# A two-layer decoder trunk: pre-norm weights as one spread row, compressed values without a masked copy, and a merged transition between the layers

## The chip, the cores and the metric

The kernel runs on one core of one Trainium2 chip. The metric is the device time of one execution in microseconds (us). Several runs are taken, and their median is given. The engines are called TensorE (PE; its weight loads PEld), VectorE (DVE), ScalarE (ACT), GpSimd (POOL) and SyncE (SP, which here only issues transfers).

## The reference

Two layers over 512 tokens of width 1024, float32. Each adds a normed mixer to its input:

```python
def rmsnorm(x, g):
    return x * lax.rsqrt(jnp.mean(x * x, axis=-1, keepdims=True) + EPS) * g

for i in range(2):
    u = rmsnorm(x, norm_pre[i])
    y = nsa_mixer(u, ...) if i == 0 else diff_mixer(u, ...)
    x = x + rmsnorm(y, norm_post[i])
```

`nsa_mixer` projects `u @ w_in` (3632 columns) into queries of 16 heads in 4 groups, three pairs of keys and values, gates and a SiLU path `z`. It adds three softmax branches (over 31 compressed blocks, over selected blocks, over a window) and ends with `@ w_out`. The compressed branch is what the change touches:

```python
p_c = softmax(where(m_c, q @ k_cmp + bias_c, NEG)) * any(m_c)
o_c = einsum('bgjqc,bcgd->bqgjd', p_c, v_cmp)
```

`diff_mixer` projects `u @ w_in` (4096 columns) into `q, k, v, z`, takes the difference of two softmax maps per head, norms per head, and ends with `@ w_out`.

## The kernel before

Tokens lie in four blocks of 128 (`NT = 4`), the width in eight blocks of 128 (`KD = 8`). A float32 product is made of three fp32r products: each operand is split into a rounded high half (`hi`, L99, an ACT copy, or a POOL operation) and a low half (`lo`, L104, a subtraction), and PE adds high x high, low x high and high x low.

Weights come through a stream (`Stream`, L108): `load` fetches a block of at most 512 KB on SP's queue into one of two `wraw` buffers, and `split` makes its halves in pieces. `split` takes the engines from `by`, two letters per piece, the first for the high half and the second for the low half (A is ACT, P is POOL, D is DVE). A block in `extra` is fetched into two `P` tiles and split into `wx` tiles. `SPD` (L43) holds the letters for the first block of `dv1`.

Projections are jobs. `mjob` gives columns x tokens. `tjob` (L205) gives tokens x columns; with `by_token` it goes through all of its weights for one token block before the next, and `evac` copies each token block's accumulator out of PSUM. Its accumulators come from PSUM banks by name: two `mm`, two `S`, three `T`, one `av`. The framework orders a writer of a bank behind earlier readers of it, also where two accumulators share the bank.

The first stage loads token block 0, the two halves of the pre-norm weights (L298, 256 KB each, one row of memory read into 128 partitions) and the first two weight blocks on SP's queue, then token blocks 1 to 3 (L610). `WARM` matmuls on a zeroed tile run meanwhile (L305). `prenorm` (L355) makes, per token block, two squares with their sums on ACT (L361), the partial sum (`part_sum`, L331), the root and one step of refinement (`row_rstd`, L340), and the normed row (L373). Its `turn` transposes the row on PE and splits it. After each token block eight steps of the job queue follow: those of `vs`, and then of `vw`.

In the attention of layer 0, `Cmp` (L881) is the compressed branch of a head group. Its `t` makes the values masked per head: a DVE multiply (L918), an ACT copy and a DVE subtraction.

The transition lies in a region where PE's order is that of the program (L1081 to L1103). The job `o1` is the second half of layer 0's output projection. When a token block of it is done, `after0` (L1065) calls `prenorm` for layer 1 with `EARLY`: there the product with the weights is POOL's (L364) and the scaling DVE's (L369). Block 1's transposes come before the last step of `o1` (`PRE1`). Then `SEQ` (L44) interleaves `dv0` (a), `dv1` (b) and the transposes of blocks 2 and 3 (p2, p3). `dv0` goes by token with two S banks for four token blocks. `tc.issue_after(i)` queues what is traced within it behind instruction `i`, on the engine of `i` and only there.

All other engines' orders, and PE's outside this region, are made by the framework at build time, by priority and a model of the times.

Of the kernel before, what the change touches and what calls it, by code (L numbers as in the profile page):

```python
# [18 lines left out]
S = 512  # L19
WARM = 7  # L20
EARLY = True
PRE1 = 29
# [20 lines left out]
SPD = ('PD',)*4  # L43
SEQ = 'a0 a1 p2 b0 b1 a2 p3 b2 a3 b3'.split()  # L44
# [24 lines left out]
def trunk(ctx: ExitStack, tc: tile.TileContext, x, table, npre, npost, w_in, pe_k, w1_k, w2_k,  # L69
# [135 lines left out]
    def tjob(name, w, width, col, n, evac, banks, cuts=((0, 4), (4, 4)), by_token=False):  # L205
        def run(i):
            bs = [bank(b) for b in banks]
            per = 4 // len(bs)
            acc = [bs[t // per][:, (t % per) * n:(t % per) * n + n] for t in range(NT)]
# [14 lines left out]
            if by_token:  # L224
                for ci in range(len(cuts)):
                    cut[ci] = ws.cut.pop(i + ci)
                for t in range(NT):
                    for ci in range(len(cuts)):
                        yield from part(ci, t)
                    evac(t, acc[t])  # L230
# [64 lines left out]
    load_x(0)  # L295
    gpre = [ptile() for _ in range(2)]
    for i in range(2):
        nc.sync.dma_start(gpre[i], drows(npre, i * 512, [[0, 128], [1, 512]]))  # L298
# [6 lines left out]
    for _ in range(WARM):  # L305
        nc.tensor.matmul(bank("T")[:, :256], BT[0][:, :128], BT[0][:, :256], start=True, stop=True)

# [47 lines left out]
    def prenorm(t, src, xn, grow, uh, ul, early):  # L355

        halves = (slice(0, 512), slice(512, 1024))
        ss = [small(1, tag="ss") for _ in range(2)]
        with tc.issue_after(T0["a"]) if "a" in T0 else ExitStack():
            for c, s in zip(halves, ss):  # L360
                nc.scalar.activation(pttile(F32) if early else xn[:, c], src[:, c], AF.Square, accum_out=s)  # L361
        if early:
            for c, g in zip(halves, grow):
                nc.gpsimd.tensor_tensor(xn[:, c], src[:, c], g, op=OP.mult)  # L364
        m0 = part_sum(ss[0])
# [9 lines left out]
        def turn():  # L375
            for i in range(2):
# [6 lines left out]
                x = hi(uh[:, i * 4:i * 4 + 4, cs], pv).ins  # L383
                T0["h"] = x
                if t == 0:
                    T0["a"] = x
# [153 lines left out]
    tjob("vs", w_in, NSA_IN, 1792, 256, evac_v(0), ("S", "S", "mm", "mm"), by_token=True)  # L540
# [50 lines left out]
    for n in range(4):  # L591
        tjob(f"dv{n}", dw_in, DIFF_IN, 2048 + n * 256, 256, evac_dv(n), (("S", "S"), ("mm", "mm"))[n % 2],
             by_token=n == 0)
# [70 lines left out]
    xn = slot("D", [128, NT, D])  # L664
# [216 lines left out]
    class Cmp:  # L881
# [22 lines left out]
        def t(self, i):  # L904
            g = self.g
            if True:
                p = bank("T")
                for qb in range(NT):
# [7 lines left out]
                vb = ptile()  # L916
                v3 = vb[:, 0:256].rearrange("p (h d) -> p h d", h=4)
                nc.vector.tensor_tensor(v3, T["vc"][:, g:g + 1, :].to_broadcast([128, 4, 64]),  # L918
                                        bmask[:, :, None].to_broadcast([128, 4, 64]), op=OP.mult)
                vt = pttile()  # L920
                hi(vt[:, 0:256], vb[:, 0:256])
                lo(vt[:, 256:512], vb[:, 0:256], vt[:, 0:256])
# [356 lines left out]
```

## Time and profile before

| | us |
|---|---|
| median of 3 runs | 663.3 |
| lowest and highest | 663.24, 665.05 |
| the profiled execution | 661.7 |
| its span, first to last instruction | 659.8 |

| engine | busy us | share of the span |
|---|---|---|
| PE | 635.3 | 96% |
| DVE | 413.7 | 63% |
| POOL | 401.3 | 61% |
| ACT | 340.3 | 52% |

Times in rows are us from the span's start. A row of the timeline names its start, its length, the engine, the line, the operation, the output and inputs with their size, the count of merged instructions, and in brackets the idle time before it with what ended it. The length of a merged row goes from the first start to the last end. A matmul's own length overlaps with its neighbours'. A row by stage gives the stretch, its length, the busy time of each engine, TensorE's granted clock as a share of 2.4 GHz, the DMA engines' busy share and GB/s.

### The profile page before, as it was taken

What the parts mean: (1) busy time and instruction counts of PE and PEld (TensorE: products, weight loads), DVE (VectorE), ACT (ScalarE), POOL (GpSimd) and SP (SyncE); (2) the same over time, 40 slices, a digit from 0 to 9 for tenths busy, and PEclk for the clock granted to TensorE, in tenths of its full rate; (3) what the DMA queues carried; (4) which work ended last, traced back from release to release, by engine and by line L of the source; (5) the groups of instructions that cost most, each with busy time, mean ns of one, the idle gap of its engine ahead of it and who ended that gap; (6) DMA issues with size and microseconds to landing.
All of it is one profiled execution on the core that took longest, in us unless ns stands there. A gap on an engine that the chain in (4) does not pass through costs nothing.

```text
span 659.8 us, 11242 instructions
## 1 busy us (share of the span) xinstructions
PE 635.3 (96%) x3773; PEld 555.5 (84%) x3773; DVE 413.7 (63%) x1188; ACT 340.3 (52%) x904; POOL 401.3 (61%) x675
## 2 busy tenths in 40 slices
PE   6999999999999999999999899999999998989996
PEld 5888888888788788888887899898987987879885
DVE  5611235678778978969878900236558668797634
ACT  6311234675767567768564311235564574668431
POOL 4778558777777587768586457948674563522300
PEclk8999999999999999999999899999999998999998
DMA  8565423213022111201852212322333232225302
GB/s 254 145 166 132 124 76 92 60 34 71 27 65 66 33 47 41 58 17 36 298 187 96 96 54 75 117 74 89 88 81 79 68 80 62 65 64 191 129 25 103
DMA packets 68989, 60.52 MB, mean 92 GB/s; under 512 B 3628, under 2 KB 60868, under 8 KB 68932
## 3 DMA queue, kind: packets, MB, share of 16 engines
q1 hardware_dynamic: 68212, 57.45, 29.9%
q10 hardware_dynamic: 720, 2.36, 0.9%
q8 instruction: 30, 0.49, 0.3%
q14 instruction: 27, 0.22, 0.1%
HBM read 55.04 MB, written 4.76 MB: 91 GB/s over the span
## 4 chain that ended last, share of the span: by engine, by line
PE 81%; DVE 11%; ACT 3%; DMA 3%; issue 2%; POOL 0%; SPq 0%; DVEq 0%; ACTq 0%; POOLq 0%
PE mm L198 31%; PE mm L218 12%; PE mm L467 6%; PE T L856 5%; PE av L870 5%; PE S L218 5%; PE S L801 4%; PE S L800 4%; PE S L467 3%; PE av L1166 2%; PE T L721 1%; DMA wraw<-in_nsa_w_in_dram 1%; PE T L1156 1%; DMA P<-in_nsa_w_out_dram 1%; DVE P L792 1%
## 5 line engine op out<-in xcount | busy, mean ns | idle before, releaser
L167 POOL TENSOR_TENSOR wlo<-wraw,whi 128x256 fp32r<-128x256 f32 (+2 forms) x247 | 184.2, 774 | 23.8 <-ACT whi L163 12.4
L165 POOL TENSOR_SCALAR whi<-wraw 128x256 fp32r<-128x256 f32 (+1 forms) x240 | 95.5, 424 | 111.9 <-PE mm L198 65.9
L794 ACT ACTIVATE P<-P,st 128x512 f32<-128x512 f32 (+3 forms) x192 | 107.5, 560 | 87.6 <-DVE st L792 86.7
L850 POOL TENSOR_SCALAR P<-P,st,gate 128x512 f32<-128x512 f32 (+3 forms) x128 | 80.1, 637 | 27.0 <-DVE st L847 24.9
L792 DVE CUSTOM_DVE_ANT_0 P<-S,BT 128x128 f32<-128x128 f32 (+2 forms) x144 | 59.7, 418 | 28.6 <-PE S L801 26.1
L198 PE MATMUL mm<-bigA,whi 128*128 128x512 f32 x192 | 77.4, 403 | 0.1
L198 PE MATMUL mm<-bigA,wlo 128*128 128x512 f32 x192 | 75.3, 392 | 0.0
L198 PE MATMUL mm<-bigB,whi 128*128 128x512 f32 x192 | 75.3, 392 | 0.0
L105 DVE TENSOR_TENSOR PT<-T,PT 128x512 fp32r<-128x512 f32 x84 | 56.9, 685 | 8.2 <-ACT PT L100 6.4
L870 PE MATMUL av<-PT,bigE 128*128 128x512 f32 x160 | 56.4, 417 | 1.2 <-DVE bigF L878 0.9
L105 DVE TENSOR_TENSOR stk<-mm,stk 64x512 fp32r<-64x512 f32 x32 | 22.0, 688 | 52.5 <-ACT stk L100 52.1
L198 PE MATMUL mm<-bigF,whi 128*128 128x512 f32 x128 | 51.9, 405 | 0.0
L856 PE MATMUL T<-ident,P 128*128 128x128 f32 x320 | 51.8, 272 | 0.0
L100 ACT ACTIVATE PT<-T 128x512 fp32r<-128x512 f32 x84 | 48.6, 592 | 6.0 <-PE T L856 3.9
L856 PEld LDWEIGHTS T<-ident,P 128*128 128x128 f32 x320 | 41.0, 140 | 12.3 <-issue 0.4
L100 ACT ACTIVATE stk<-mm 64x512 fp32r<-64x512 f32 x64 | 37.8, 591 | 25.8 <-PE mm L198 14.9
L198 PE MATMUL mm<-bigE,whi 128*128 128x512 f32 x128 | 50.8, 397 | 0.0
L198 PE MATMUL mm<-bigF,wlo 128*128 128x512 f32 x128 | 50.7, 396 | 0.0
L218 PE MATMUL mm<-whi,bigF 128*128 128x256 f32 x176 | 50.3, 287 | 0.1
L218 PE MATMUL mm<-wlo,bigF 128*128 128x256 f32 x176 | 50.0, 285 | 0.0
L218 PE MATMUL mm<-whi,bigE 128*128 128x256 f32 x176 | 49.6, 283 | 0.0
L198 PEld LDWEIGHTS mm<-bigB,whi 128*128 128x128 f32 x192 | 36.1, 188 | 8.1
(288 smaller groups left out, 1650.8 us busy)
## 6 DMA issues: line engine op xcount, KB each, us to landing
wraw<-in_diff_w_in_dram SPq DMA_DIRECT2D x31, 512.0 KB, 3.9
wraw<-in_nsa_w_in_dram SPq DMA_DIRECT2D x26, 512.0 KB, 4.1
BT<-rd SPq DMA_DIRECT2D x32, 128.0 KB, 3.4
wraw<-in_diff_w_out_dram SPq DMA_DIRECT2D x5, 512.0 KB, 4.0
bigF<-in_x_dram SPq DMA_DIRECT2D x4, 512.0 KB, 9.5
wraw<-in_nsa_w_out_dram SPq DMA_DIRECT2D x4, 512.0 KB, 3.4
bigD<-in_x_dram SPq DMA_DIRECT2D x4, 512.0 KB, 3.7
x1d<-bigD ACTq DMA_DIRECT2D x4, 512.0 KB, 4.9
```

Source lines behind the costliest of these rows:

```text
L100: return nc.scalar.activation(dst, src, AF.Copy, scale=scale)
L105: nc.vector.tensor_tensor(dst, src, h.bitcast(F32), op=OP.subtract)
L165: nc.gpsimd.tensor_scalar(h[:, a:b], v, 1.0, 0.0, op0=OP.mult, op1=OP.add)
L167: e.tensor_tensor(l[:, a:b], v, h[:, a:b].bitcast(F32), op=OP.subtract)
L198: T["mm"] = nc.tensor.matmul(p[:, a:b], wt[:, k, :], u[:, k, a:b], start=(k == 0 and j == 0), stop=(k == KD - 1 and j == 2)).ins
L218: nc.tensor.matmul(acc[t], u[:, k0 + k, t * 128:(t + 1) * 128], wt[:, k, :], start=(ci == 0 and k == 0 and j == 0 and t % per == 0), stop= ...
L467: nc.tensor.matmul(p, U[u][:, k, t * 128:(t + 1) * 128], wt[wi], start=start and j == 0, stop=stop and j == 2, skip_group_check=True)
L792: nc.vector.tensor_tensor_reduce(out=o, in0=i0, in1=b, op0=OP.add, op1=OP.min, scale=-1.0, scalar=BIG, accum_out=nm)
L794: nc.scalar.activation(pt[:, :n], pt[:, :n], AF.Exp, bias=nm, scale=-1.0, accum_out=den)
L850: NORM(nc, i, br, qb).tensor_scalar(self.P[i][:, :n], self.P[i][:, :n], st[:, 8 + i:9 + i], gate[:, NT - 1 - qb, c:c + 1], op0=OP.mult, op ...
L856: T["tmark"] = nc.tensor.transpose(p[:, j * 128:(j + 1) * 128], self.P[j][:, kb * 128:(kb + 1) * 128], ident).ins
L870: nc.tensor.matmul(av, T["V"][:, br, kb, g, :], p, start=(br == 0 and kb == 0 and j == 0), stop=(br == 1 and kb == qb and j == 1))
```

## The change

First stage: the pre-norm weights come as one row of 4 KB into partition 0 of the tile `xn`, through ACT's queue. Two matmuls with a row of ones spread it into the two `mm` banks, from which the multiply (L373) reads it. Token block 0 comes in two transfers. Two warm-up matmuls are left of seven. From block 1 on, one square of 1024 columns replaces two, and its partial sum falls away. `vs` takes its accumulators one at a time, all from the S banks.

Compressed values: four ACT copies scaled by a column of the mask and four DVE operations, each of 64 columns, replace the masked copy and its split.

Transition: the high halves of `dv1`'s first block go from POOL to ACT, the low ones from DVE to POOL. Block 1's transposes move from within `o1` to the head of `SEQ`. `dv0` has a bank of its own for each token block (S, T, S, S). POOL's work traced in the region is queued behind the last multiply (L364). The rule that queues later squares on ACT behind the split of block 0 is dropped.

```diff
--- before.py
+++ after.py
@@ -17,9 +17,8 @@
 AX = mybir.AxisListType
 
 S = 512
-WARM = 7
+WARM = 2
 EARLY = True
-PRE1 = 29
 ZE = 'gpsimd', 'vector'
 OB = (2,2,2)
 LAG = 1
@@ -40,8 +39,8 @@
 OPRE = 0
 ODELAY = 0
 QN = 1
-SPD = ('PD',)*4
-SEQ = 'a0 a1 p2 b0 b1 a2 p3 b2 a3 b3'.split()
+SPD = ('AP',)*4
+SEQ = 'p1 a0 a1 p2 b0 b1 a2 p3 b2 a3 b3'.split()
 PRE = {16: 2, 24: 3}
 SPX = ('AP',) * 4
 SPN = 2
@@ -204,9 +203,12 @@
 
     def tjob(name, w, width, col, n, evac, banks, cuts=((0, 4), (4, 4)), by_token=False):
         def run(i):
-            bs = [bank(b) for b in banks]
-            per = 4 // len(bs)
-            acc = [bs[t // per][:, (t % per) * n:(t % per) * n + n] for t in range(NT)]
+            if by_token:
+                per, acc = 1, [None] * NT
+            else:
+                bs = [bank(b) for b in banks]
+                per = 4 // len(bs)
+                acc = [bs[t // per][:, (t % per) * n:(t % per) * n + n] for t in range(NT)]
             cut = {}
 
             def part(ci, t):
@@ -225,6 +227,7 @@
                 for ci in range(len(cuts)):
                     cut[ci] = ws.cut.pop(i + ci)
                 for t in range(NT):
+                    acc[t] = bank(banks[t])[:, :n]
                     for ci in range(len(cuts)):
                         yield from part(ci, t)
                     evac(t, acc[t])
@@ -292,10 +295,13 @@
     def load_x(t):
         nc.sync.dma_start(xt[:, t, :], drows(x, t * 128 * D, [[D, 128], [1, D]]))
 
-    load_x(0)
-    gpre = [ptile() for _ in range(2)]
+    xn = slot("D", [128, NT, D])
+    grow = xn[0:1, NT - 1]
+    nc.scalar.dma_start(grow, drows(npre, 0, [[D, 1], [1, D]]))
     for i in range(2):
-        nc.sync.dma_start(gpre[i], drows(npre, i * 512, [[0, 128], [1, 512]]))
+        nc.sync.dma_start(xt[:, 0, i * 512:i * 512 + 512], drows(x, i * 512, [[D, 128], [1, 512]]))
+    ones = const.tile([1, 128], F32, name="ones")
+    nc.vector.memset(ones, 1.0)
     BTN = 256 + 4 * 384
     BT = [const.tile([128, BTN], F32, name=f"BT{i}") for i in range(2)]
     for t in BT:
@@ -304,6 +310,9 @@
     make_identity(nc, ident)
     for _ in range(WARM):
         nc.tensor.matmul(bank("T")[:, :256], BT[0][:, :128], BT[0][:, :256], start=True, stop=True)
+    gpre = [bank("mm") for _ in range(2)]
+    for i in range(2):
+        nc.tensor.matmul(gpre[i], ones, grow[:, i * 512:i * 512 + 512], start=True, stop=True)
 
     def rsqrt(y, ss, n, scale):
 
@@ -355,14 +364,15 @@
     def prenorm(t, src, xn, grow, uh, ul, early):
 
         halves = (slice(0, 512), slice(512, 1024))
+        whole = t and not early
         ss = [small(1, tag="ss") for _ in range(2)]
         with tc.issue_after(T0["a"]) if "a" in T0 else ExitStack():
-            for c, s in zip(halves, ss):
+            for c, s in ((slice(0, D), ss[1]),) if whole else zip(halves, ss):
                 nc.scalar.activation(pttile(F32) if early else xn[:, c], src[:, c], AF.Square, accum_out=s)
         if early:
             for c, g in zip(halves, grow):
-                nc.gpsimd.tensor_tensor(xn[:, c], src[:, c], g, op=OP.mult)
-        m0 = part_sum(ss[0])
+                T["xm"] = nc.gpsimd.tensor_tensor(xn[:, c], src[:, c], g, op=OP.mult).ins
+        m0 = epst if whole else part_sum(ss[0])
         if early:
             r, q = row_rstd(m0, ss[1], split=True)
             for c in halves:
@@ -380,10 +390,7 @@
                     nc.tensor.transpose(p[:, j * 128:(j + 1) * 128], xn[:, k * 128:(k + 1) * 128], ident)
                 pv = p.rearrange("p (j c) -> p j c", j=4)
                 cs = slice(t * 128, (t + 1) * 128)
-                x = hi(uh[:, i * 4:i * 4 + 4, cs], pv).ins
-                T0["h"] = x
-                if t == 0:
-                    T0["a"] = x
+                T0["h"] = hi(uh[:, i * 4:i * 4 + 4, cs], pv).ins
                 lo(ul[:, i * 4:i * 4 + 4, cs], pv, uh[:, i * 4:i * 4 + 4, cs])
         return turn
 
@@ -537,7 +544,7 @@
         ws.extra |= set(range(j.first + 1, j.first + 4))
         ws.quick |= set(range(j.first - (QN if early else 4), j.first + 4))
 
-    tjob("vs", w_in, NSA_IN, 1792, 256, evac_v(0), ("S", "S", "mm", "mm"), by_token=True)
+    tjob("vs", w_in, NSA_IN, 1792, 256, evac_v(0), ("S", "S", "S", "S"), by_token=True)
     tjob("vw", w_in, NSA_IN, 2304, 304, evac_v(1), ("mm", "mm", "S", "S"), cuts=((0, 3), (3, 3), (6, 2)))
     mjob("kc0", w_in, NSA_IN, 1024, evac_cmp("kcs", 0))
     mjob("kc1", w_in, NSA_IN, 1152, evac_cmp("kcs", 2))
@@ -589,8 +596,8 @@
         tjob(f"dz{n}", dw_in, DIFF_IN, 3072 + n * 256, 256, evac_dz(n), ("mm", "mm"))
 
     for n in range(4):
-        tjob(f"dv{n}", dw_in, DIFF_IN, 2048 + n * 256, 256, evac_dv(n), (("S", "S"), ("mm", "mm"))[n % 2],
-             by_token=n == 0)
+        tjob(f"dv{n}", dw_in, DIFF_IN, 2048 + n * 256, 256, evac_dv(n),
+             (("S", "T", "S", "S"), ("mm", "mm"), ("S", "S"), ("mm", "mm"))[n], by_token=n == 0)
     dqk(0)
     dz(0)
     dqk(1)
@@ -661,7 +668,6 @@
     T["gate"] = gate
     U["h"] = slot("A", [128, KD, S], F32R)
     U["l"] = slot("B", [128, KD, S], F32R)
-    xn = slot("D", [128, NT, D])
     for t in range(NT):
         prenorm(t, xt[:, t], xn[:, t], gpre, U["h"], U["l"], False)()
         for _ in range(8):
@@ -913,13 +919,11 @@
                 hi(ph, p)
                 lo(pl, p, ph)
                 self.pt = (ph, pl)
-                vb = ptile()
-                v3 = vb[:, 0:256].rearrange("p (h d) -> p h d", h=4)
-                nc.vector.tensor_tensor(v3, T["vc"][:, g:g + 1, :].to_broadcast([128, 4, 64]),
-                                        bmask[:, :, None].to_broadcast([128, 4, 64]), op=OP.mult)
                 vt = pttile()
-                hi(vt[:, 0:256], vb[:, 0:256])
-                lo(vt[:, 256:512], vb[:, 0:256], vt[:, 0:256])
+                for h in range(4):
+                    a, b, m = vt[:, 64 * h:64 * h + 64], vt[:, 256 + 64 * h:320 + 64 * h], bmask[:, h:h + 1]
+                    hi(a, T["vc"][:, g], m)
+                    nc.vector.scalar_tensor_tensor(b, T["vc"][:, g], m, a.bitcast(F32), op0=OP.mult, op1=OP.subtract)
                 self.vt = vt
 
         def v(self, c):
@@ -1078,24 +1082,21 @@
     T["wx"] = wx_ctx.enter_context(tc.tile_pool(name="wx", bufs=1))
     with tc.manual_schedule(engines={mybir.EngineType.PE}):
         run.upto("oC")
-        while run.i <= index["o1"]:
-            run.step()
-            if run.done - T.setdefault("o1b", run.done) > PRE1 * 640:
-                if ("pre", 1) in T:
-                    T.pop(("pre", 1))()
+        run.upto("o1")
         T["dv"] = slot("A", [128, NT, D])
         U["h"], U["l"] = U1["h"], U1["l"]
         ws.split()
         gens = [jobs[index[n]].run(jobs[index[n]].first) for n in ("dv0", "dv1")]
-        for w in SEQ:
-            if w[0] == "p":
-                T["pre", int(w[1])]()
-            else:
-                for _ in range({"a": 8, "b": 4}[w[0]]):
-                    next(gens["ab".index(w[0])], None)
-        for g in gens:
-            for _ in g:
-                pass
+        with tc.issue_after(T["xm"]):
+            for w in SEQ:
+                if w[0] == "p":
+                    T["pre", int(w[1])]()
+                else:
+                    for _ in range({"a": 8, "b": 4}[w[0]]):
+                        next(gens["ab".index(w[0])], None)
+            for g in gens:
+                for _ in g:
+                    pass
         run.i = index["dv2"]
         run.done += 2 * jobs[index["dv0"]].cost
     wx_ctx.close()
```

## Rows read from the trace of the kernel before

**Rows 1.** The page's first part: busy us, share, instructions of each engine

```profile
PE 635.3 (96%) x3773; PEld 555.5 (84%) x3773; DVE 413.7 (63%) x1188; ACT 340.3 (52%) x904; POOL 401.3 (61%) x675
```

**Rows 2.** Stages: PE, PEld, DVE, ACT, POOL busy (count), clock, DMA share, GB/s

```profile
4.30:11.10 6.80, 3.18 (x18) 2.21 (x16) 2.76 (x9) 3.52 (x12) 1.53 (x3) 1.00 1.00 331
11.10:14.60 3.50, 3.36 (x16) 3.07 (x16) 3.35 (x8) 3.07 (x11) 3.50 (x6) 0.51 0.76 249
...
19.27:43.05 23.78, 23.78 (x183) 23.78 (x184) 9.03 (x19) 6.16 (x14) 14.71 (x27) 1.00 0.58 155
358.00:364.20 6.20, 5.23 (x27) 4.00 (x26) 6.17 (x15) 1.12 (x4) 6.20 (x13) 1.00 0.03 13
364.20:369.69 5.49, 3.04 (x25) 2.82 (x24) 5.49 (x9) 3.63 (x11) 3.92 (x3) 0.99 0.57 184
369.69:374.10 4.41, 4.41 (x25) 4.41 (x26) 4.40 (x16) 0.64 (x2) 0.59 (x1) 0.63 0.02 8
```

**Rows 3.** PE's waits in the whole trace: total us, times, longest

```profile
PE S L218 <- ACT bigA L571: 2.4, 1, 2.4
...
PE T L380 <- DVE bigC L369: 1.0, 1, 1.0
PE av L870 <- DVE bigF L878: 0.9, 1, 0.9
```

**Rows 4.** The chain that ended last, first stage: start, us, what

```profile
2.12 6.86 DMA wraw<-in_nsa_w_in_dram
```

**Rows 5.** Timeline of the first stage

```profile
1.19 4.82 PE L306 MATMUL T<-BT 128*128 128x256 f32 x14 [1.19 <-DVE BT L302]
1.19 0.89 SPq L298 DMA_DIRECT2D P<-in_norm_pre_dram  x2
...
6.63 1.61 DVE L373 SCALAR_TENSOR_TENSOR bigD<-bigF,rstd,P 128x512 f32<-128x512 f32 x2
...
13.57 0.29 ACT L345 ACTIVATE rstd<-ss,m 128x1 f32<-128x1 f32 x1 [0.43 <-DVE m L335]
```

**Rows 6.** Stages, columns as in the second group, while the transfers run

```profile
3.00:6.00 3.00, 3.00 (x11) 2.15 (x9) 0.48 (x4) 1.63 (x5) 0.00 (x0) 1.00 0.92 207
7.00:11.00 4.00, 1.38 (x9) 0.97 (x10) 1.28 (x3) 1.99 (x6) 1.44 (x3) 1.00 1.08 397
```

**Rows 7.** Transfers of the whole trace: issues, KB each, median us to landing

```profile
lams<-in_diff_lambda_q_dram SPq DMA_DIRECT2D x2, 32.0 KB, 3.0
...
bigF<-in_nsa_cmp_w_k_dram SPq DMA_DIRECT2D x1, 0.5 KB, 6.5
```

**Rows 8.** By line: a DVE subtraction that reads PSUM, busy us, mean ns

```profile
L105 DVE TENSOR_TENSOR PT<-T,PT 128x512 fp32r<-128x512 f32 x84 | 56.9, 685 | 8.2 <-ACT PT L100 6.4 <-PE av L870 1.3
```

**Rows 9.** The chain in the transition: PE on one token block

```profile
369.69 4.56 PE S L218 x24
...
377.99 2.88 PE S L218 x24
```

**Rows 10.** Timelines of the transition, DVE, then ACT, then POOL

```profile
365.47 3.26 DVE L160 TENSOR_TENSOR wx<-P,wx 128x256 fp32r<-128x256 f32 x3
...
369.28 0.36 ACT L571 ACTIVATE bigA<-S 128x256 f32<-128x256 f32 x1
...
361.31 1.85 POOL L159 TENSOR_SCALAR wx<-P 128x256 fp32r<-128x256 f32 x4
...
364.96 3.15 POOL L364 TENSOR_TENSOR bigC<-bigD,P 128x512 f32<-128x512 f32 x2
```

**Rows 11.** Low halves by line: ns min/median/max, first and last start

```profile
L160 POOL TENSOR_TENSOR bigC<-wraw,bigC x6: 722/729/919, 9.6 to 14.1; 128x256 fp32r<-128x256 f32 x6
L160 DVE TENSOR_TENSOR wx<-P,wx x4: 409/949/1518, 365.5 to 368.7; 128x256 fp32r<-128x256 f32 x4
```

**Rows 12.** Masked copy, and an operation of 64 columns: columns as above

```profile
L918 DVE TENSOR_TENSOR P<-vcmp,bmask x4: 440/1791/3137, 160.3 to 319.9; 128x256 f32<-128x256 f32 x4
...
L1111 DVE CUSTOM_DVE_ANT_0 lams<-lams x2: 320/346/371, 340.5 to 341.1; 128x64 f32<-128x64 f32 x2
```

## The prediction

> **What bounds the kernel now.** First the page's busy row: TensorE (PE) is busy 96% of the span [rows 1], so only time in which PE is idle, or runs at the lower clock, can be taken out. The table by stage then says where such time lies. In 4.30 to 11.10 us PE is busy 3.18 us; from 11.10 to 14.60 its mean clock is 0.51; from 19.27 to 43.05 it is busy without a hole. In 364.20 to 369.69 it is busy 3.04 of 5.49 us, and in the 4.41 us after that the mean clock is 0.63 [rows 2]. Those are the two places that the diff touches, beside the compressed branch. Third, the list of who waited for whom: in the second place PE waits 2.4 us for the copy of `dv0`'s first accumulator (L571) and 1.0 us for a token block's normed row (L369) [rows 3].
>
> The profiled execution took 661.7 us, 1.9 us more than its span of 659.8 us, and 1.6 us less than the median of the three runs (663.3 us). The gain is worked out in its trace and then subtracted from the median.
>
> **First stage.** The chain opens with the first weight block's transfer, 2.12 to 8.98 us [rows 4]. Ahead of that block on SP's queue stand token block 0 and, at 1.19 us, the two pre-norm halves, each spread over 128 partitions by its transfer [rows 5]. While these moved, in 3 to 6 us, the DMA engines were busy to 0.92 but moved 207 GB/s; in 7 to 11 us, with ordinary blocks, 397 GB/s [rows 6]. The halves are 2 x 256 KB: at the later rate 0.52 MB / 397 GB/s = 1.3 us. The slow stretch moved 0.62 MB in 3.0 us where 1.6 us would have done: another 1.4 us. I take 2.7 us, by which the weights and token blocks 1 to 3 land earlier; the lower bound is 1.3 us, if the slowness has another cause. Every later step of the stage starts from these landings: the weights' split, block 1's square, PE's dense stretch.
>
> One square of 1024 columns in place of two of 512, for blocks 1 to 3, drops a DVE add (L335) between the last square and the square root. ScalarE (ACT) waited 0.43 us there for it [rows 5]. I count 0.3 us, since part of that is the hand-over, which stays. Together 3.0 us.
>
> Added are one row of 4 KB through ACT's queue, a memset, and two matmuls of 512 columns from one partition. Seven such f32 matmuls of 256 columns are 14 instructions in 4.82 us, 0.34 us each [rows 5]; two of 512 columns are four of 0.69 us, 2.75 us. The row's landing isn't in this trace. The nearest rows are 3.0 us from issue (32 KB, later) and 6.5 us (0.5 KB behind full queues) [rows 7]. Issued at about 1 us like SP's, with only block 0 ahead of it, it lands by the first at 4.0, and the weights stand in PSUM at 6.7 us, against a multiply that began at 6.63 us [rows 5]: no delay. By the second they stand there at 10.3 us, 3.6 us late. The multiply now reads the weights from PSUM. From SBUF it takes 0.81 us [rows 5], a DVE operation of that size that reads PSUM 0.69 us [rows 8]: no term, bounds of 0.1 us for each of 8 both ways. Block 0's transfer in halves brings its first square forward, which nothing waits for while the weights land later: no term.
>
> Five warm-up matmuls go; the broadcasts take their place in time. In the trace the clock fell at 11.10 after PE had been busy 3.18 of 6.80 us, and was back at 14.60 [rows 2]. What the new order makes of it can go both ways: 24 matmuls of a token block cost 4.56 us where the clock was low and 2.88 us where it was high [rows 9], so 1.7 us either way, taken as nothing.
>
> The Trainium skill ("TensorE: Matmul & The Clock Gate", section "What's actually happening") says that the throttled state is the default and that activity releases it, which speaks against dropping warm-up work. By it block 0 would cost those 1.7 us again, and the forecast would be 657.5 us.
>
> First stage: -3.0 us, between 0 (the row late) and -4.7 us (the clock kept).
>
> **Transition.** Before, VectorE (DVE) made the low halves of `dv1`'s first weight block (three of the four in 3.26 us from 365.47), and block 2's partial sum stood behind them. ACT's square root waited for that sum, and on ACT, which works in order, `dv0`'s evacuation (369.28) stood behind the square root [rows 10]. PE's token block 1 shared the bank with block 0 and waited for that evacuation. The diff breaks this twice: the low halves go to GpSimd (POOL), and each token block of `dv0` has a bank of its own. The wait of 2.4 us goes [rows 3], and so does the low clock behind it, 4.56 - 2.88 = 1.7 us [rows 9]. Block 1's transposes move from before the last step of `o1` to behind it. Of their wait of 1.0 us [rows 3] the three matmuls of that step then cover 3 x 512 columns, 0.7 us by 2.88 us for 24 of 256 [rows 9]. I count 0.6 us. Sum 2.4 + 1.7 + 0.6 = 4.7 us.
>
> What is late next: block 2's transposes. They began where the last stretch of [rows 2] ends, 374.10 us, and PE would now reach them at 369.4 us. They need POOL's multiply of block 2 (364.96 to 368.11) and after it DVE's scaling. POOL drops the four high halves (1.85 us) and gets four low ones of 0.73 to 0.92 us, 2.9 to 3.7 us [rows 10, 11]. So its multiply ends 1.1 to 1.8 us later, at 369.2 to 369.9 us, and the second half's scaling, an operation of some 0.7 us like the one of [rows 8], at about 370.4. The first four transposes need only the first half. I take 0.4 us of wait, bounds 0 and 2.0. The four high halves on ACT (4 x 0.36 us, as an ACT copy of that size [rows 10]) lie in its idle time before 364.2, where it is busy 1.12 of 6.20 us [rows 2], and cost 1.4 us if that cover is gone. The moved step issues no DMA. POOL's splits of `dv2`'s weights are queued behind its last multiply, and POOL had room there: busy 0.59 of 4.41 us [rows 2]. Transition: -4.3 us, between -1.0 (with the clock falling again) and -5.1 us.
>
> **Compressed values.** Per head group a DVE multiply (0.44 to 3.14, median 1.79 us [rows 12]), an ACT copy of 256 columns (0.36 us) and a DVE subtraction (at least that multiply's 0.44 us) become four ACT copies and four DVE operations of 64 columns. Such a DVE operation took 0.35 us [rows 12], so DVE goes from 2.2 to 1.4 us. An ACT operation of 64 columns lies between one column, 0.29 us [rows 5], and 256, 0.36 us: four are 1.2 to 1.4 us, 0.8 to 1.1 us more. In groups 0 to 2 both lie beside PE's work. In the last group they lie on the way to the `o` projection; PE once waited 0.9 us for a DVE copy that stands behind this multiply (L878) [rows 3]. I take -0.2 us, bounds -0.9 and +1.1 us.
>
> **Sum.** 3.0 + 4.3 + 0.2 = 7.5 us: the profiled execution would go from 661.7 to 654.2 us, the median from 663.3 to **655.8 us**. Where PE is dense a shift of its work is kept to the end.
>
> **The rivals.** (B) Only the transition pays: the row lands late and its 3.6 us eat the 3.0 us. For it: no row of the trace shows such a transfer at this place. Against: the 6.5 us are from full queues. 663.3 - 4.3 - 0.2 = 658.8 us.
>
> (C) POOL takes DVE's place in the transition. Where both work both are slower: DVE's low halves took 0.41 to 1.52 us, POOL's 0.72 to 0.92 us [rows 11]. If PE waits 2.0 us at block 2's transposes, the clock falls as before (1.7 us), and 4.7 - 3.7 = 1.0 us is left: 663.3 - 3.0 - 1.0 - 0.2 = 659.1 us. Against it: the first half of the block is enough to start. The Trainium skill ("SBUF — State Buffer", section "Who interferes with whom") states that a DVE instruction with two SBUF inputs and a GpSimd one that reads SBUF contend through a shared read interface; it speaks for this rival.
>
> (D) The change does not do what it says: the weights' landing is set by something else than the halves, and the transposes wait as long as the evacuation did. About 663 us.
>
> (E) Slower: `vs` keeps only the two S banks, because the mm banks hold the pre-norm weights until block 3's multiply. Each token block must then wait for the evacuation of the one two before. A wait of that kind cost 2.4 us in `dv0` [rows 3]. Four of them (`vs` 2 and 3, `vw` 2 and 3) and one fall of the clock are 9.6 + 1.7 = 11.3 us, so 663.3 - 7.5 + 11.3 = 667.1 us; it decides from 7.5 us on. Against it: the 24 matmuls of the block between take 2.88 us [rows 9], more than such a wait.
>
> **How the numbers follow.** Forecast 0.68, B 0.12, C 0.10, D 0.06, E 0.04. About 0.3%, 2 us, is what a measurement of this kernel can tell from no change. The forecast, B and C are faster by more (0.90), D is the same (0.06), E slower (0.04). The forecast's own range is 653 to 658.5 us. To hold 8 in 10 the range reaches up past B and C to 660.0; below, both stages at their better bound give 663.3 - 4.7 - 5.1 - 0.2 = 653.3, or 652.8 with half of the third term's.
>
> **What would show it.** Right: no broadcast transfer at 1.19 us; the first weights land near 6.3 us; PE is dense from about 16.3 us; the stage that ended at 43.05 ends at about 40; no PE wait on L571 and no half clock near 370 us; block 2's transposes some 7.4 us earlier than 374.1. Wrong: PE waits for the broadcasts or an S bank before 25 us, or for L369 by more than 2 us at block 2; or the gain is there at 40 and 366 us and gone at the end.

## The result, and the profile after

The kernel before took 663.27 us (median of four runs of that comparison, 662.78 to 665.05), the changed one 655.68 us (654.73 to 658.39). The ratio is 0.9887, 95% interval 0.9853 to 0.9922. The profiled execution of the changed kernel took 655.29 us, its span is 653.3 us; before they were 661.7 and 659.8. The forecast was 655.8 us, so the sum came out. Its terms did not.

The page of the changed kernel, busy us by engine, answers to [rows 1]:

```profile
PE 635.7 (97%) x3767; PEld 554.5 (85%) x3767; DVE 406.2 (62%) x1190; ACT 344.7 (53%) x914; POOL 401.4 (61%) x675
```

PE's busy time is what it was; what fell is the time around it. The list of waits of the changed kernel, beside [rows 3]:

```profile
PE T L220 <- DVE bigE L104: 1.0, 1, 1.0
...
PE S L220 <- DVE rs L358: 0.7, 1, 0.7
...
PE T L390 <- DVE rstd L361: 0.3, 1, 0.3
```

The 2.4 us behind the evacuation are gone. In their place PE waits 1.0 us for the low half of block 1 (L104). Stages of the changed kernel, columns as in [rows 2]: the transfers, PE's start, the rest of the first stage, and the transition from block 1's transposes to block 2's:

```profile
3.00:6.00 3.00, 3.00 (x4) 1.16 (x4) 0.44 (x3) 1.74 (x5) 0.00 (x0) 1.00 0.86 271
...
9.62:15.10 5.48, 5.14 (x22) 4.85 (x23) 4.95 (x16) 4.49 (x10) 4.02 (x8) 1.00 0.75 231
15.39:41.51 26.12, 25.12 (x195) 24.68 (x193) 10.27 (x21) 7.86 (x17) 12.25 (x24) 1.00 0.54 146
...
359.43:368.24 8.81, 7.38 (x57) 6.77 (x58) 7.73 (x20) 3.64 (x11) 3.52 (x3) 1.00 0.15 60
```

The second row is the first surprise: 22 matmuls take 5.14 us, and the clock's column says 1.00. That column has no record in this trace before 15 us; the pace of the matmuls shows the lower clock, as the timeline of PE in the changed kernel does:

```profile
1.31 2.08 PE L312 MATMUL T<-BT 128*128 128x256 f32 x4 [1.31 <-DVE BT L308]
3.32 3.78 PE L315 MATMUL mm<-bigD,ones 1*128 1x512 f32 x4
7.66 1.94 PE L390 MATMUL T<-ident,bigD 128*128 128x128 f32 x8 [0.56 <-DVE bigD L383]
...
14.76 0.41 PE L220 MATMUL S<-bigC,bigB 128*128 128x256 f32 x1
...
15.27 0.28 PE L220 MATMUL S<-bigC,bigB 128*128 128x256 f32 x1
```

A matmul of 256 columns takes 0.41 us up to 14.76 and 0.28 from 15.27 on. So in this execution TensorE came to 2.4 GHz only at about 15 us.

All kernels of this study by the same landmarks, in us: the start of the first weights' split on ACT; the first matmul of `kc0`; the attention of layer 0 from its first score to the last group's compressed product; the transition from block 0's to block 2's transposes; the rest to the end; the span.

| kernel | split | kc0 | attention | transition | rest | span |
|---|---|---|---|---|---|---|
| before | 9.01 | 42.89 | 216.99 | 18.45 | 285.72 | 659.8 |
| changed | 6.95 | 41.51 | 215.16 | 15.42 | 285.04 | 653.3 |
| e1_first | 6.85 | 40.19 | 217.05 | 18.30 | 285.70 | 657.1 |
| e2_cmp | 9.48 | 43.38 | 215.14 | 18.66 | 285.68 | 658.6 |
| e3_trans | 8.80 | 42.72 | 216.97 | 15.42 | 284.45 | 655.4 |
| e4_warm7 | 6.86 | 46.05 | 215.11 | 15.41 | 285.88 | 658.6 |
| e5_after | 6.90 | 42.30 | 215.18 | 15.40 | 285.31 | 654.3 |
| e6_seq | 6.85 | 41.19 | 215.09 | other order | 285.28 | 653.0 |
| e7_spd | 7.46 | 41.77 | 215.07 | 13.62 | 286.33 | 653.0 |
| e8_bank | 7.27 | 40.94 | 215.13 | 15.42 | 284.44 | 651.6 |
| e9_warm5 | 6.89 | 45.13 | 215.13 | 13.62 | 284.50 | 654.5 |
| e10_p1old | 7.67 | 41.29 | 215.04 | 14.73 | 285.57 | 652.4 |
| e11_spd | 7.61 | 42.05 | 215.16 | 13.62 | 284.32 | 651.3 |
| e12_neither | 6.81 | 41.34 | 215.18 | 14.63 | 285.54 | 652.5 |

e7_spd, e8_bank, e10_p1old and e12_neither ran once each, for their traces. The columns for the attention and the transition repeat within 0.4 us wherever a kernel has the same code there, so a single trace settles a question of half a microsecond in them. `kc0` and the rest do not repeat: one and the same stage gives 41.51 and 42.30. The rest is 284.3 to 284.5 us where the clock stayed up from the transition to the last 10 us, 285.0 to 285.9 where it fell there once, 286.3 where it fell twice. No edit of the change lies there.

From before to changed: first stage -1.38, attention -1.83, transition -3.03, rest -0.68, and 0.4 us given back between attention and transition (in some of these kernels, not in others). Sum -6.5 us.

### The profile page after: what moved, and what is told of

The parts are those of the page before. It is cut to its first block, busy times and chain, and to the rows that moved or that the text cites. A ratio compares the mean times of both kernels' runs of the same rounds, so it can differ in the third digit from the quotient of the medians.

```text
span 653.3 us, 11250 instructions
## 1 busy us (share of the span) xinstructions
PE 635.7 (97%) x3767; PEld 554.5 (85%) x3767; DVE 406.2 (62%) x1190; ACT 344.7 (53%) x914; POOL 401.4 (61%) x675
## 4 chain that ended last, share of the span: by engine, by line
PE 85%; DVE 8%; ACT 3%; issue 2%; DMA 1%; SPq 0%; DVEq 0%; ACTq 0%
PE mm L197 31%; PE mm L220 12%; PE mm L474 6%; PE S L220 6%; PE av L876 6%; PE T L862 5%; PE S L807 4%; PE S L806 4%; PE S L474 3%; PE av L1167 2%; PE T L727 1%; PE T L1157 1%; DMA wraw<-in_nsa_w_in_dram 1%; DVE stk L104 1%; DVE P L798 1%
## 5 line engine op out<-in xcount | busy, mean ns | idle before, releaser
L104 DVE TENSOR_TENSOR PT<-T,PT 128x512 fp32r<-128x512 f32 x84 | 56.9, 685 | 7.3 <-ACT PT L99 5.0
L104 DVE TENSOR_TENSOR stk<-mm,stk 64x512 fp32r<-64x512 f32 x32 | 22.0, 689 | 52.2 <-ACT stk L99 51.8
```

The costliest lines, as they stand in the source:

```text
L104: nc.vector.tensor_tensor(dst, src, h.bitcast(F32), op=OP.subtract)
```

## The experiments

**One part alone.** Three kernels, each the kernel before with one part of the change. None of their three ratios is clear of 1 in its interval; what they tell, their traces tell.

e1_first has the row, the broadcasts, block 0 in halves, two warm-ups, the single squares and `vs` on the S banks:

```diff
-    load_x(0)
-    gpre = [ptile() for _ in range(2)]
...
+    nc.scalar.dma_start(grow, drows(npre, 0, [[D, 1], [1, D]]))
...
+        nc.tensor.matmul(gpre[i], ones, grow[:, i * 512:i * 512 + 512], start=True, stop=True)
```

> The kernel before with the first-stage edits alone (weights as one row spread by two matmuls, block 0 in halves, one square of 1024 columns, vs on the S banks, two warm-up matmuls). Theory P (the sizes of the prediction): 663.3 - 3.0 = 660.3 us. Theory S (sizes read from the two traces, where the stage that ended at 43.05 us ends at 41.67): about 661.9 us, the first token block at half clock until about 15 us.

It took 660.24 us beside 661.93 for the kernel before (ratio 0.9982, 0.9960 to 1.0004). In its trace the first weights are split 2.2 us earlier and `kc0` begins 2.7 us earlier; its pace changes at 13.4 us. So in one execution the first stage gave nearly what was forecast.

e2_cmp has the compressed values alone:

```diff
-                nc.vector.tensor_tensor(v3, T["vc"][:, g:g + 1, :].to_broadcast([128, 4, 64]),
...
+                    hi(a, T["vc"][:, g], m)
+                    nc.vector.scalar_tensor_tensor(b, T["vc"][:, g], m, a.bitcast(F32), op0=OP.mult, op1=OP.subtract)
```

> The kernel before with the compressed values made without the masked copy, and nothing else. Theory P: 663.3 - 0.2 = 663.1 us. Theory S: the shift between the two traces grows by 1.4 us between 43 and 350 us, where only this edit lies, so about 661.9 us.

It took 660.74 us (ratio 0.9982, 0.9957 to 1.0007). The attention is 1.85 us shorter, and so it is in every kernel that has this edit. The timeline of DVE, then of PE, in the kernel before shows where half of that was lost:

```profile
214.45 3.14 DVE L918 TENSOR_TENSOR P<-vcmp,bmask 128x256 f32<-128x256 f32 x1
217.51 0.84 DVE L878 TENSOR_TENSOR bigF<-av,PT 64x256 f32<-64x256 f32 x2
...
218.49 1.16 PE L870 MATMUL av<-PT,bigE 128*128 128x512 f32 x4 [0.91 <-DVE bigF L878]
```

The multiply is not needed until the end of its group, but the copy that frees the bank `av` stands behind it on DVE, and PE's next product needs the bank: 0.91 us. All of PE's waits in the attention, before, and then in the changed kernel:

```profile
PE av L870 <- DVE bigF L878: 0.9, 1, 0.9
PE S L800 <- DVE st L792: 0.8, 2, 0.5
PE T L910 <- DVE PT L105: 0.4, 2, 0.2
PE av L870 <- DVE PT L105: 0.2, 1, 0.2
...
PE S L806 <- DVE st L798: 0.8, 2, 0.5
PE T L935 <- ACT PT L99: 0.2, 1, 0.2
PE S L935 <- DVE st L798: 0.2, 1, 0.2
```

PE's idle time there falls from 2.49 to 1.35 us, by 1.1 of the 1.83 us. The other 0.7 us shows in no wait, and where it comes from stays open. The new operations, four to a group, are short (by line, in the changed kernel):

```profile
L926 DVE SCALAR_TENSOR_TENSOR PT<-vcmp,bmask,PT 128x64 fp32r<-128x64 f32 x16 | 3.7, 282 | 0.5 <-ACT PT L99 0.5
```

None of them holds the queue for long.

e3_trans has the transition's edits alone (`SPD`, `SEQ`, the banks of `dv0`, the queueing of POOL's work):

```diff
-SPD = ('PD',)*4
-SEQ = 'a0 a1 p2 b0 b1 a2 p3 b2 a3 b3'.split()
+SPD = ('AP',)*4
+SEQ = 'p1 a0 a1 p2 b0 b1 a2 p3 b2 a3 b3'.split()
...
+        with tc.issue_after(T["xm"]):
```

> The kernel before with the transition edits alone. Theory P: 663.3 - 4.3 = 659.0 us. Theory S: between block 0's transposes and block 2's the shift grows by 2.9 us, and by 0.8 us after it, so 659.6 to 660.4 us, with a wait of about 1 us of token block 1 for DVE's low half.

It took 659.7 us (ratio 0.9975, 0.9950 to 1.0001); the transition takes 15.42 us instead of 18.45, as in the changed kernel. In this trace the first stage is as before and the clock doesn't fall in it, yet `kc0` begins only 0.17 us earlier. The three traces of the old stage show why: `kc0` begins 33.88 (before), 33.90 (e2) and 33.92 us (e3) after the first weights' split, though the clock is low for 3.4, 6.8 and 0 us of it. PE waits for block 1's normed row in any case (0.38 us before, 0.77 in e3). Where the landings set the pace, half clock cost nothing.

**Warm-ups back.** e4_warm7 is the changed kernel with seven warm-up matmuls:

```diff
-WARM = 2
+WARM = 7
```

> The changed kernel with seven warm-up matmuls in place of two. Theory S says that the broadcasts from one partition do not keep the clock up and the missing warm-up costs the first token block 24 matmuls at half clock: with seven the clock is raised near 4.3 us as before, the broadcasts run at full clock, and the time is 1 to 2 us less than that of the changed kernel, 654 to 655 us. Rival: the seven stand ahead of the broadcasts on PE, which end later, and the time is the same or up to 1 us more (655.7 to 656.7 us).

It took 659.11 us (ratio 0.9956, 0.9936 to 0.9977), slower than the changed kernel, and `kc0` begins at 46.05 us. PE, then DVE, in its first stage:

```profile
4.96 1.98 PE L315 MATMUL mm<-bigD,ones 1*128 1x512 f32 x4
...
8.26 0.60 PE L390 MATMUL T<-ident,bigD 128*128 128x128 f32 x4
10.87 0.63 PE L390 MATMUL T<-ident,bigD 128*128 128x128 f32 x4 [2.01 <-DVE bigD L383]
...
6.14 0.75 DVE L383 SCALAR_TENSOR_TENSOR bigD<-bigF,rstd,mm 128x512 f32<-128x512 f32 x1
8.78 1.29 DVE L159 TENSOR_TENSOR bigC<-wraw,bigC 128x256 fp32r<-128x256 f32 x2 [1.89 <-ACT bigC L99]
9.99 0.73 DVE L383 SCALAR_TENSOR_TENSOR bigD<-bigF,rstd,mm 128x512 f32<-128x512 f32 x1
```

The clock did come up: the same four broadcasts take 1.98 us instead of 3.78, four transposes 0.60 instead of about 1. But with more warm-ups ahead the framework put the weights' low halves (L159), which wait for ACT, between the two halves of block 0's product (L383), and PE waited 2 us for the second. The clock then fell again: it is 0.50 from 11.7 to 21.8 us. The run tells of an order, and nothing of what the clock is worth.

So e9_warm5 writes the order out, with five warm-ups and the split of e7 (below):

```diff
-WARM = 2
+WARM = 5
...
+            with tc.issue_after(x):
+                for low in T0.pop("late", ()):
+                    low()
...
+                if t == 0 and not early:
+                    T0["a"] = T0["h"]
```

> The kernel of e7 with five warm-up matmuls, and with the order that e4 lost written out: the second weight block's low halves on DVE are queued behind block 0's product, and the later squares on ACT behind block 0's split, as in the kernel before. Theory: in the changed kernel the first stage gave 1.4 us instead of 2.7 because TensorE did little before 7.6 us and its matmuls went at the low clock's pace (0.21 us from start to start) until 13.4 to 15.9 us. With the clock up earlier the first kc0 matmul stands at 40.0 to 40.5 us instead of 41.2 to 42.3, and the time falls by 1 to 1.5 us against the kernel of e7. Rival: block 1's normed row is what is late, the clock costs nothing, and PE waits for that row; kc0 at 41.2 us or later and the time as in e7.

It took 656.0 us beside 653.9 for e11_spd in the same rounds (ratios to before 0.9918, 0.9896 to 0.9940, and 0.9898, 0.9869 to 0.9926), and `kc0` begins at 45.13. The theory fell. PE in its first stage:

```profile
1.31 3.78 PE L316 MATMUL T<-BT 128*128 128x256 f32 x8 [1.31 <-DVE BT L312]
5.02 3.78 PE L319 MATMUL mm<-bigD,ones 1*128 1x512 f32 x4
...
9.74 1.91 PE L397 MATMUL T<-ident,bigD 128*128 128x128 f32 x8
...
19.21 0.63 PE L397 MATMUL T<-ident,bigD 128*128 128x128 f32 x4 [1.47 <-DVE bigD L387]
```

PE begins with the same eight warm-up instructions as in e4_warm7 and goes on without a hole, but the broadcasts run at 1.2 GHz here (0.95 us each) and at 2.4 GHz there. The pace changes only at 13.4 us, and the clock is low again (0.50) from 20.3 to 23.5 us. The warm-ups only pushed the broadcasts 1.7 us back, and with the order that was written out block 2's normed row came late (1.47 us). Whether the clock comes up early is not set by this stretch of PE's work alone; what else sets it is open.

**The changed kernel again**, in the rounds of the next experiment:

> The changed kernel itself once more, in the same rounds as the next one. By the theory that its first stage gained only 1.4 us in its first trace because the granted clock rose late there (15.1 us), the gain at the first kc0 matmul (42.89 us before) differs from execution to execution: where the clock rises earlier it is 2.5 to 3.0 us, kc0 near 40 us. By the rival, that the new order itself costs 1.3 us beside the halves, kc0 stands at 41.3 to 41.7 us again. The transition doesn't depend on this: from block 0's to block 2's transposes 15.4 us again, with 1.0 us of PE's wait for block 1's low half.

It took 656.34 us (ratio 0.9899, 0.9873 to 0.9924). `kc0` begins at 42.30: the gain in the first stage was 0.6 us in this execution, by neither expectation. The pace changes later here, at 15.9 us. Over the nine traces with this first stage and its order, those of e4 and e9 left out, `kc0` lies between 40.19 and 42.30, median 41.34; over the three with the old stage between 42.72 and 43.38, median 42.89. The two ends of the first group are traces in which the pace changes at 13.4 and 15.9 us; in e11_spd it changes last, at 16.4, with `kc0` at 42.05. The pace is not the whole of it: in e5_after PE also waits 0.91 us for block 0's low half, in the first trace 0.34. The closest pair is e1_first and e12_neither, where block 0's matmuls begin at 9.45 and 9.52 us, the pace changes at 13.4 and 15.6, and `kc0` begins at 40.19 and 41.34.

**Another sequence.** e6_seq puts a step of `dv1` between block 1's transposes and their use:

```diff
-SEQ = 'p1 a0 a1 p2 b0 b1 a2 p3 b2 a3 b3'.split()
+SEQ = 'p1 a0 b0 a1 p2 b1 a2 p3 b2 a3 b3'.split()
```

> SEQ begins p1 a0 b0 a1 p2 b1 a2 instead of p1 a0 a1 p2 b0 b1 a2: a step of dv1 for token block 0 (12 matmuls, 1.44 us) lies between block 1's transposes and its use. Theory: block 1's low half on DVE is what is late, so the 1.0 us of wait before a1 goes, and block 3's transposes follow block 0's in 21.0 us instead of 22.04; time 0.9 us less than the changed kernel. Rival: block 2's low half becomes late in its place, since only one such step is left between its transposes and a2: a wait of about 0.6 us there, 21.6 us or more, and the time falls by 0.3 us or nothing.

It took 655.98 us (0.9905, 0.9873 to 0.9937), the changed kernel's time. PE in its transition:

```profile
359.33 1.17 PE L390 MATMUL T<-ident,bigC 128*128 128x128 f32 x8 [0.80 <-DVE bigC L379]
...
371.74 0.39 PE L220 MATMUL S<-whi,bigE 128*128 128x256 f32 x1 [0.89 <-DVE bigE L104]
```

The wait before `a1` went and came back before `a2`, as the rival had it, at 0.89 us. From block 0's to block 3's transposes it takes 22.42 us against 22.04 in the changed kernel.

**The transition's edits, undone one by one.** The forecast counted on two of them, the low halves' engine and the banks. e7_spd undoes the first, e8_bank the second, e12_neither both, e10_p1old the place of block 1's transposes.

```diff
-SPD = ('AP',)*4
+SPD = ('PD',)*4
```

> The changed kernel with the first block of dv1 split as before: high halves on POOL, low halves on DVE. PE's order is the same, and each token block of dv0 keeps a bank of its own. Theory: DVE's in-order queue sets block 2's scaling and block 1's low half, so 3.3 to 3.8 us of low halves ahead of them come back as waits: PE waits again 1.0 us or a little more for block 1's low half and 1 to 3 us for block 2's transposes; block 0's to block 2's transposes take 17 to 18.5 us instead of 15.4. Rival: the banks alone took the wait away, and the split's engine is nothing: 15.4 us again.

The rival was nearer, and even it fell short: the transition takes 13.62 us, 1.8 less than with the edit. e11_spd is the same kernel, timed:

> The kernel of e7, timed: the changed kernel with the first block of dv1 split by POOL and DVE as before. By e7's trace its transition is 1.8 us shorter than the changed kernel's (13.6 us from block 0's to block 2's transposes), so the time should be 1 to 2 us below the changed kernel's (656.0 us in its two sets of runs), near 654.5 us; the ratio to the kernel before near 0.987. If the 1.8 us were an accident of one execution, 15.4 us would come back.

It took 653.9 us beside 661.3 before; the ratio of 0.9898 can't be told from the changed kernel's 0.9899 and 0.9887. The trace repeats to the hundredth: 13.62 us again. DVE, POOL and PE in e7_spd:

```profile
358.48 1.00 DVE L379 TENSOR_SCALAR bigC<-bigC,rstd,rs 128x512 f32<-128x512 f32 x2
359.40 0.42 DVE L159 TENSOR_TENSOR wx<-P,wx 128x256 fp32r<-128x256 f32 x1
...
359.81 1.09 DVE L159 TENSOR_TENSOR wx<-P,wx 128x256 fp32r<-128x256 f32 x3
...
362.14 0.68 DVE L104 TENSOR_TENSOR bigE<-T,bigF 128x512 fp32r<-128x512 f32 x1
...
356.66 1.51 POOL L158 TENSOR_SCALAR wx<-P 128x256 fp32r<-128x256 f32 x4 [0.81 <-PE S L474]
361.64 2.98 POOL L374 TENSOR_TENSOR bigC<-bigD,P 128x512 f32<-128x512 f32 x2 [3.47 <-DVE bigD L1056]
...
366.64 1.08 PE L390 MATMUL T<-ident,bigC 128*128 128x128 f32 x8 [0.50 <-DVE bigC L379]
```

The low halves are back on DVE and harmless. They begin at 359.40, right behind block 1's scaling, and take 1.5 us in all, while POOL stands idle from 358.2 to 361.6. Before, they began at 365.47, beside POOL's multiply, and three of them took 3.26 us [rows 10]. Block 1's low half comes at 362.14 and PE doesn't wait for it; the one wait left is block 2's 0.50 us.

```diff
-             (("S", "T", "S", "S"), ("mm", "mm"), ("S", "S"), ("mm", "mm"))[n], by_token=n == 0)
+             (("S", "S"), ("mm", "mm"), ("S", "S"), ("mm", "mm"))[n], by_token=n == 0)
```

> The changed kernel with two token blocks of dv0 to a bank again (S, S), so that block 1 must wait for block 0's evacuation. The low halves stay on POOL. Theory: with the split off DVE the evacuation (365.08 us in the changed kernel) comes ahead of block 1's low half (366.5 us), so the shared bank costs nothing at this place: block 0's to block 2's transposes take 15.4 to 15.7 us. Rival: the bank is what the change gains by, and the wait of 2.4 us comes back: 17 us or more.

15.42 us, the changed kernel's. A wait for the evacuation is there again, but it takes the place of the one for the low half (PE in e8_bank):

```profile
364.07 0.39 PE L220 MATMUL S<-whi,bigF 128*128 128x256 f32 x1 [1.25 <-ACT bigA L579]
```

> The changed kernel with both undone that e7 and e8 undid one at a time: the first block of dv1 split by POOL and DVE as before, and dv0's token blocks two to a bank. What stays of the transition's edits is the place of block 1's transposes and of POOL's later work. Theory: these place the low halves ahead of block 2's work on DVE (359.4 to 360.8 us in e7), and the evacuation then ends at 364.6 us where PE needs it at 363.1: a wait of 1.5 us in place of 0.5 for block 2, 14.5 to 14.8 us from block 0's to block 2's transposes, against 18.45 before. Rival: the split and the bank each bring the gain and one of the two is enough, so with neither the old wait of 2.4 us or more and some 17 to 18.5 us are back.

With both edits undone at once the transition takes 14.63 us, 3.8 us less than before and 0.8 less than with both. POOL, DVE, then PE in e12_neither:

```profile
355.91 1.52 POOL L158 TENSOR_SCALAR wx<-P 128x256 fp32r<-128x256 f32 x4 [0.81 <-PE S L475]
...
358.66 0.42 DVE L159 TENSOR_TENSOR wx<-P,wx 128x256 fp32r<-128x256 f32 x1
...
363.94 0.39 PE L220 MATMUL S<-whi,bigF 128*128 128x256 f32 x1 [1.42 <-ACT bigA L579]
```

The expectation held to 0.1 us. So neither of the two edits is needed for the gain. Of the 3.8 us, 1.0 is the shorter wait for the evacuation (1.42 us instead of 2.44), 1.4 the 24 matmuls behind it, which go at full clock (2.97 us instead of 4.40), and 1.0 the wait ahead of block 1's transposes, which is gone. What is left of the change here is the queueing of POOL's work and the place of block 1's transposes. The dropped rule on ACT can't be it: `after0` empties `T0` (L1066) before each `prenorm` of layer 1, so that the rule never held there; it held in the first stage. POOL's order in the kernel before names the queueing (POOL, then PE):

```profile
358.43 1.52 POOL L165 TENSOR_SCALAR whi<-wraw 128x256 fp32r<-128x256 f32 x4
359.91 1.44 POOL L167 TENSOR_TENSOR wlo<-wraw,whi 128x256 fp32r<-128x256 f32 x2
...
387.33 0.28 PE L218 MATMUL mm<-whi,bigF 128*128 128x256 f32 x1
```

These are splits of `dv1`'s second block, which PE first reads at 387.33. They stood ahead of the high halves of its first block, which began at 361.31 [rows 10], 5.7 us after block 0's transposes; in e12_neither they begin 3.6 us after them. The low halves come after the high ones, and block 2's sum, ACT's root and the evacuation after the low ones.

The transposes' place is the other candidate:

```diff
-        run.upto("o1")
+        while run.i <= index["o1"]:
+            run.step()
+            if run.done - T.setdefault("o1b", run.done) > 29 * 640:
...
```

> The changed kernel with block 1's transposes back ahead of the last step of o1. By the prediction the move is worth 0.6 us, so block 0's to block 2's transposes take 16.0 us instead of 15.4. Rival: the transposes' start is set by DVE's scaling and the step that follows them by DVE's low half, so the wait ahead of the transposes grows by up to 0.7 us, the wait for the low half (1.0 us) shrinks by the same, and the stretch takes 15.4 us again.

With the transposes back ahead of the last step of `o1` the transition takes 14.73 us, 0.7 less than in the changed kernel, by neither expectation. PE waits once (e10_p1old):

```profile
359.36 1.17 PE L390 MATMUL T<-ident,bigC 128*128 128x128 f32 x8 [1.46 <-DVE bigC L379]
```

The wait ahead of the transposes is longer, but the matmuls behind it now cover block 1's split, and the 1.0 us for the low half is gone. So beside the other edits this one costs and doesn't gain; with the old split and banks (e12_neither) it may carry part of the 1.0 us ahead of the transposes. The queueing of POOL's work alone was not tried. It is the one edit that all kernels with the gain share; that it carries the gain is argued from that and from the order of the rows, and not shown.

## Why the prediction was right, and where it was not

**The sum** held by luck, because errors offset each other: first stage -1.4 instead of -3.0, transition -3.0 instead of -4.3, attention -1.8 instead of -0.2, 0.4 given back, and -0.7 in the rest, where the clock fell once in both traces but at another place, and which nothing in the change accounts for. Of the signs named, PE no longer waits on L571 and the clock stays up near 370 us, but `kc0` begins at 41.51 and not at about 40, and block 2's transposes come 5.9 us earlier and not 7.4.

**First stage.** The mechanism was right. The halves' transfers are gone, 271 GB/s flow in 3 to 6 us where 207 did [rows 6], and the first weights' split begins 1.3 to 2.2 us earlier; 2.7 was too much. The row came by 3.32 us (4.0 was the better bound), so rival B is out. The multiply from PSUM takes 0.70 us, within its bounds. PE waits for no `vs` bank, so rival E is out. The 0.3 us for the single squares no run shows by itself. The other term that failed is the clock, "taken as nothing". The broadcasts took 0.95 us each, not 0.69, the transposes 1.94 us, and 22 of the first 24 matmuls went at the lower pace. In the old stage the clock had cost nothing; here block 0's matmuls run without a gap into block 1's transposes at 15.39, so the pace counts. How much is not shown in full. Block 1's normed row is ready at 14.68, 0.7 us before those transposes, and matmuls that ended sooner would have waited for it. DVE in the changed kernel:

```profile
13.27 1.41 DVE L383 SCALAR_TENSOR_TENSOR bigD<-bigF,rstd,mm 128x512 f32<-128x512 f32 x2
```

In the closest pair above the pace changes 2.2 us later and `kc0` comes 1.15 us later. What the stage takes with an early rise and this order no run shows, so the price of 1.7 us stays open.

The Trainium skill ("TensorE: Matmul & The Clock Gate", section "What's actually happening") has the throttled state as the default, released by activity; with 657.5 us the prediction gave the time by it. The start of these traces agrees: PE came up at the lower pace in every one. That more warm-up work brings the clock up early fits too: in the four traces with seven warm-ups (before, e2, e3, e4) it rose at 4.3, 7.1, 6.4 and 4.8 us, in the ten with two or five at 13.4 us or later. But it is not the instructions ahead of the rise alone: the same eight stand at the start of e4_warm7 (up at 4.8) and of e9_warm5 (13.4). Whether seven would have made this kernel faster is not shown, since e4 changed the order with them.

**Transition.** The 2.4 us and the fall behind them went, as forecast. But the step "the diff breaks this twice" named the wrong edits: e7, e8 and e12 show that neither was needed beside the others. The low halves' engine costs 1.8 us where the banks are separate (15.42 against 13.62) and 0.8 where they are shared (15.42 against 14.63); the banks bring 1.0 us, and only while the engine is DVE. POOL's later splits, queued behind its last multiply, were taken for those of `dv2` and weighed as a cost with room for them; they are those of `dv1`'s second block, and by the order of the rows they had made the low halves late. The 0.6 us for block 1's transposes had the wrong sign beside the other edits (e10: 0.7 us lost). And what was late next was not block 2 (0.4 us) but block 1's low half (1.00 us). DVE in the changed kernel:

```profile
361.89 0.15 DVE L344 TENSOR_SCALAR m<-ss 128x1 f32<-128x1 f32 x1
362.93 1.26 DVE L355 SCALAR_TENSOR_TENSOR rs<-ss,m 128x1 f32<-128x1 f32 x1 [0.88 <-ACT PT L371]
364.11 0.68 DVE L461 TENSOR_TENSOR bigC<-S,P 128x512 f32<-128x512 f32 x1
364.71 0.14 DVE L355 SCALAR_TENSOR_TENSOR rs<-ss,m 128x1 f32<-128x1 f32 x1
364.77 1.27 DVE L104 TENSOR_TENSOR bigE<-T,bigF 128x512 fp32r<-128x512 f32 x2
```

The low half stands behind block 2's sum. That sum is one column and took 1.26 us while POOL's multiply ran (361.18 to 364.17), 0.14 after it. Rival C, in which POOL's work slows DVE's, was right in kind and small in size. The rule that the prediction set beside it, from the Trainium skill ("SBUF — State Buffer", section "Who interferes with whom"), that a DVE instruction with two SBUF inputs contends with a GpSimd one that reads SBUF, agrees with the low halves: three took 3.26 us beside POOL [rows 10] and 1.09 us while POOL was idle. It agrees with the sum as well: the operation on one column with one input (L344) took 0.15 us beside the same multiply.

**Compressed values.** The sizes were right (DVE 0.28 us an operation, 0.35 forecast) and the place was wrong. "In groups 0 to 2 both lie beside PE's work" looked at when the values are needed, not at what stands behind the multiply on DVE. The row for it was there [rows 3], and was put to the last group; it lies at 218.49 us, in the middle. It is half of the gain: 0.7 us of the 1.83 show in no wait.

## What to carry to other kernels

Before an operation is called hidden, look at what stands behind it on its engine: a 3 us operation that nobody needs yet made PE wait for the copy behind it. When several edits attack one wait, undo them one by one and then together: here one brought its 1.0 us only without another, that other cost 0.8 to 1.8 us, a third cost 0.7 beside them, and the one that looked like bookkeeping, the order of POOL's later work, is the likeliest to carry the gain, and should have been run alone. And when the transfers stop setting the pace of a stage, TensorE's clock can begin to count: it cost nothing in the old first stage and 1.15 us in the closest pair of the new one.

## What the runs showed of the hardware that was not expected

The clock's column can be 1.00 for want of a record: from 0 to 15 us of the changed kernel only the matmuls' pace (0.41 against 0.28 us, broadcasts 0.95 against 0.49) shows 1.2 GHz. An operation on one column with two SBUF inputs on DVE took 1.26 us beside POOL's multiply and 0.14 us without it. And the moment at which the clock comes up differs between two executions of one kernel by 0.8 us (15.1 and 15.9), of another by 1.1 us (e7_spd, 15.3, and e11_spd, 16.4), and by 8 us between two kernels whose PE began alike.
